# Gated linear attention: next pair's projections issued among this pair's heads, q, f and v in two buffers, merge gates kept in DRAM

## The chip, the cores and the metric

One Trainium2 chip, one core used. The metric is the device time of one execution in microseconds (us); the kernel before was run three times: median 4328.0 us, 4326.5 to 4329.1 us.

## The reference, cut to what matters

The program is two transformer blocks on 512 tokens of width 1024. The change lies in the second block's token mixer, which runs a delta-rule branch (finished before the changed code) and then the gated linear attention below, and merges the two:

```python
h = _modulate(_rmsnorm(x, norm1_w), sh1, sc1)          # 512 x 1024; hc: the same for 256 context tokens
qkv, ga, ab, qb, fb2, ib, gb, mg = split(h @ w_in)      # qb, ib, gb 1024 wide, fb2 and mg 2048
# _hgrn2_branch: 8 heads of 128, chunks of 64, forwards and backwards, context first
q = silu(qb); v = ib
f = lb + (1 - lb) * sigmoid(fb2);  logf = log(f);  k = 1 - f
bc = cumsum(logf, within a chunk)
scores = (q * exp(bc - ref)) @ (k * exp(ref - bc)).T, lower triangle
o = scores @ v + (q * exp(bc)) @ S;  S = exp(bc_last) * S + (k * exp(bc_last - bc)).T @ v
o = rmsnorm(o_forward + o_backward) * silu(gb)
# merge
g_a, g_b = split(sigmoid(mg));  mix = (g_a * (oa @ w_pa) + g_b * (ob @ w_pb)) @ w_o
```

## The kernel before, in words

All products of this stage are float32 split in a high and a low part, three matmuls for one (mm3, L308). `proj2` (L1208) projects the 512 tokens (and the 256 of the context where they are asked for) to up to 256 columns of w_in: it loads the weights through SP in pieces of 128x512 into three buffers w_raw (L1221), casts a piece to w_hi on ACT (L1224), subtracts on DVE, or on the engine given as `lo_eng`, to w_lo (L1225), both in two buffers, and accumulates in banks of a pool of four (`psa`): one bank for each 128 columns and one for the context. Then it evicts through a function that is handed in. `proj` (L313) is the same for 512 columns at once, in all four banks; of its w_lo pieces (L293) every fourth is done by POOL, the others by DVE.

`gla` (L1668) works on four pairs of heads (hg). For a pair it projects q (evicted with a tanh), the two directions' f (evicted by ACT as a sigmoid out of PSUM, L1711 and L1712, then scaled by DVE, L1713), takes the logarithms (L1732, four of 128x768, kept in the order of the code on ACT) and 1 - f (POOL, L1733), and projects v, which is transposed to token order. q, f and v have one buffer each. Then come the pair's two heads, and in each two directions d, four turns (j, d) in all. A turn scans the logarithms on DVE (L1755), makes the scaled copies of q and k (ACT's exponentials, POOL's L1764 and L1783, DVE's L1765), the scores, the transposed k, and runs a chain of 11 products and updates of the state S (PE L1811, DVE L1817). After two turns the head's output is summed (L1824, L1828), normalised on DVE (L1833 to L1839: gl_y), transposed (L1844), and multiplied by the gate, whose projection g is called once in a pair, after gl_y of head j = 0. At the end `split` makes obh and obl (ACT L274, DVE L275). After both heads `between(hg)` projects a quarter of the merge's gates, four tiles of 128x512 evicted with a tanh (L1906) which stay in SBUF, 16 tiles in all.

`block2_merge` (L1912) loads the delta-rule branch's output (oar, SP L1921), splits it (oah, oal), projects it with w_pa and ob with w_pb, and multiplies each result in PSUM by its gate (L1936, L1940).

The order of the code is not the order of issue: the framework (below: the planner) hands each engine its instructions beforehand in a fixed order, taking what it reckons ready, the code's order deciding between ready ones. `keep_in_program_order` pins an instruction behind the one that stands before it in the code on the same engine. Pools opened with `side="right"` share their memory with the right-hand pools opened after them, a tile of the new pool waiting for the last use of the old tiles that lie there.

Of the kernel before, what the change touches and what calls it, by code (L numbers as in the profile page):

```python
# [9 lines left out]
F32 = mybir.dt.float32  # L10
# [4 lines left out]
AF = mybir.ActivationFunctionType  # L15
ALU = mybir.AluOpType
# [4 lines left out]
P = 128  # L21
D = 1024
S = 512
# [155 lines left out]
class Net:  # L179
# [725 lines left out]
    def between(self):  # L905
        self.n_between += 1
        if self.n_between % 3 == 0:
            self.load_expert()
# [759 lines left out]
    def gla(self, acts, keep, between):  # L1668


        nc, a = self.nc, self.a
# [3 lines left out]
        main, ctx = acts  # L1675
        nw, ol, lb = self.gla_nw, self.gla_ol, self.gla_lb
        with ExitStack() as st:
# [19 lines left out]
            for hg in range(4):  # L1697
                q, f, gate = [], [[], []], []

                def q_ev(j, ps, pc):  # L1700
                    t = pool.tile([P, S], F32, tag=f"q{j}", name=f"glq{j}")
                    tc = self.to_cols(t)
                    nc.scalar.activation(out=tc, in_=self.by_rows(ps), func=AF.Tanh, scale=0.5)
                    stt(tc, tc, 1.0, self.by_rows(ps), op0=ALU.add, op1=ALU.mult)
                    q.append(t)

                def f_ev(d):
                    def g(j, ps, pc):
                        h = hg * 2 + j
                        t = pool.tile([P, 768], F32, tag=f"f{d}{j}", name=f"glf{d}{j}")  # L1710
                        nc.scalar.activation(out=self.to_cols(t[:, 0:512]), in_=self.by_rows(ps), func=AF.Sigmoid)  # L1711
                        nc.scalar.activation(out=t[:, 512:768], in_=pc, func=AF.Sigmoid)  # L1712
                        ts(t, t, ol[:, h:h + 1], lb[:, h:h + 1], op0=ALU.mult, op1=ALU.add)  # L1713
                        f[d].append(t)
                    return g

# [6 lines left out]
                self.proj2(4128 + hg * 256, 256, (main, None), q_ev)  # L1723
                self.proj2(5152 + hg * 256, 256, (main, ctx), f_ev(0))
                self.proj2(6176 + hg * 256, 256, (main, ctx), f_ev(1))

                lf = [[], []]
                for j in range(2):
                    for d in range(2):
                        t = tp.tile([P, 12, 64], F32, tag=f"lf{d}{j}", name="gl_lf", bufs=1)  # L1730
                        self.tc.keep_in_program_order(
                            nc.scalar.activation(out=t.rearrange("p c i -> p (c i)"), in_=f[d][j], func=AF.Ln))  # L1732
                        pts(f[d][j], f[d][j], -1.0, 1.0, op0=ALU.mult, op1=ALU.add)  # L1733
                        lf[d].append(t)

                v = pool.tile([P, 6, 256], F32, tag="v", name="glv")

                def v_ev(j, ps, pc):
                    t = tp.tile([P, 768], F32, tag="vT", name="gl_vT", bufs=1)
                    nc.scalar.copy(self.to_cols(t[:, 0:512]), self.by_rows(ps))  # L1740
                    nc.vector.tensor_copy(t[:, 512:768], pc)
                    for b0, nb in ((0, 4), (4, 2)):
                        pt = self.pt("pt_v")
                        for b in range(nb):
                            nc.tensor.transpose(pt[:, b * P:(b + 1) * P], t[:, (b0 + b) * P:(b0 + b + 1) * P], self.ident)
                        nc.vector.tensor_copy(v[:, b0:b0 + nb, j * P:(j + 1) * P], pt[:, :nb * P].rearrange("p (b c) -> p b c", c=P))
                self.proj2(7200 + hg * 256, 256, (main, ctx), v_ev)
                for j in range(2):
                    h = hg * 2 + j
                    Sst, qd = [], []  # L1750
                    for d in range(2):
# [66 lines left out]
                        Sst.append(S8)  # L1818
                    ss = tp.tile([P, 768], F32, tag="vT", name="gl_scs", bufs=1)[:, :512].rearrange("p (b i) -> p b i", b=NB)
# [30 lines left out]
                between(hg)  # L1850
# [39 lines left out]
    def block2_mix(self):  # L1890

        a, st, hT, hcT = self.a, self.st2, self.hT2, self.hcT
        oa_d = self.dram.tile([8, P, S], F32, name="oa_d")
        self.stx.close()
        self.banks(4, 0, 4)
        with self.pool("gdp") as gp:
            self.gdn((hT, hcT), gp, oa_d)

        self.banks(4, 2, 2)
        mgates = [[], [], [], []]  # L1900
        mp = st.enter_context(self.pool("mgp"))

        def merge_gates(n):
            def ev(j, ps):
                t = mp.tile([P, S], F32, name=f"mgate{n}{j}")
                self.nc.scalar.activation(out=self.to_cols(t), in_=self.by_rows(ps), func=AF.Tanh, scale=0.5)  # L1906
                mgates[n].append(t)
            self.proj(a["w_in_2"][0], 9248 + (n % 2) * 1024 + (n // 2) * 512, hT, True, ev)
        ob = self.gla((hT, hcT), mp, merge_gates)
        return st, mgates, oa_d, ob, self.xres  # L1910

    def block2_merge(self, st, mgates, oa_d, ob, xres):  # L1912
# [6 lines left out]
        for n in range(8):  # L1919
            raws.append(mr.tile([P, S], F32, tag=f"m2h{n}", name=f"oar{n}"))  # L1920
            nc.sync.dma_start(out=raws[n], in_=oa_d[n])  # L1921

# [500 lines left out]
```

## Time and profile before

| | |
|---|---|
| three runs | 4326.5, 4328.0, 4329.1 us |
| the profiled execution, its own time | 4329.5 us |
| its span, first to last instruction of the program | 4327.5 us |
| PE busy | 4021.8 us (93%) |
| DVE busy | 2740.9 us (63%) |
| ACT busy | 1682.5 us (39%) |
| POOL busy | 1156.9 us (27%) |

The span is what the trace covers; 2.0 us of the execution lie around it. Times in rows are counted from the span's start. A busy time counts when an engine works on an instruction; matmuls overlap, so a busy PE still has a clock that may be full (1.00) or half (0.50). Gated linear attention takes the stretch from about 2267 to 2793 us; the merge follows.

### The profile page before, as it was taken

Reading aid. Unit: us, or ns where it says so; the run is one execution under the profiler, and the core shown is the slowest. Engines: PE = TensorE matmul, PEld = TensorE weight load, DVE = VectorE, ACT = ScalarE, POOL = GpSimd, SP = SyncE. Lnnn points to the kernel's source line nnn. Section 1 sums busy time; section 2 is a strip of 40 time slices with the busy share of each in tenths; the row PEclk is TensorE's granted clock in tenths of the full one; section 3 lists DMA queues with packets and bytes.
Section 4 is the critical chain, followed back from the end, with each engine's and each line's share of the span. In section 5 each row is a group of like instructions: output and inputs, shape, how many; then the busy total and the mean of one; then the engine's idle time right before and its main releaser. Section 6 shows DMA issues by size and latency. Waiting matters only on the chain. (4 is left out here: it accounts for less than half of the span.)

```text
span 4327.5 us, 59112 instructions
## 1 busy us (share of the span) xinstructions
PE 4021.8 (93%) x21308; PEld 3134.1 (72%) x21309; DVE 2740.9 (63%) x6166; ACT 1682.5 (39%) x3200; POOL 1156.9 (27%) x1094
## 2 busy tenths in 40 slices
PE   8999899999998998899889899898789899999998
PEld 6677644767774456678777777676689799899886
DVE  5455455553644565777765655536989777777776
ACT  4544211544441144445543444323256333333333
POOL 2001100100021014222111211125779244444443
PEclk9999999999999998999989999999999999999999
DMA  4144698222458961212212111243145988888875
GB/s 137 30 121 141 248 419 357 91 79 81 112 190 329 420 245 49 65 49 57 57 46 57 47 52 52 66 127 117 59 161 198 331 310 293 302 295 301 289 267 195
DMA packets 342588, 739.72 MB, mean 171 GB/s; under 512 B 72513, under 2 KB 175025, under 8 KB 314641
## 3 DMA queue, kind: packets, MB, share of 16 engines
q1 hardware_dynamic: 277536, 540.54, 37.4%
q0 software_dynamic: 45376, 167.76, 10.4%
q10 hardware_dynamic: 19376, 27.57, 1.8%
q8 instruction: 171, 2.80, 0.3%
q14 instruction: 129, 1.05, 0.1%
HBM read 694.07 MB, written 41.70 MB: 170 GB/s over the span
## 5 line engine op out<-in xcount | busy, mean ns | idle before, releaser
L308 PE MATMUL acc<-rn_hi,w_lo 128*128 128x512 f32 x1224 | 506.7, 415 | 41.5 <-DVE w_lo L1225 15.2
L308 PE MATMUL acc<-rn_hi,w_hi 128*128 128x512 f32 x1224 | 507.7, 415 | 23.0 <-ACT w_hi L1224 13.2
L308 PE MATMUL acc<-rn_lo,w_hi 128*128 128x512 f32 x1224 | 500.9, 409 | 2.0 <-POOL rn_lo L275 2.0
L293 POOL TENSOR_TENSOR w_lo<-w_raw,w_hi 128x512 fp32r<-128x512 f32 x103 | 135.8, 1319 | 1041.4 <-ACT w_hi L291 828.4
L2246 ACT CAST p_hi<-p_raw 128x1024 fp32r<-128x1024 f32 x256 | 268.3, 1049 | 329.7 <-PE pu L308 236.3
L308 PE MATMUL pu<-rn_hi,p_lo 128*128 128x384 f32 x1024 | 349.7, 342 | 20.3 <-POOL p_lo L2247 16.0
L291 ACT CAST w_hi<-w_raw 128x512 fp32r<-128x512 f32 x316 | 196.0, 622 | 440.9 <-PE acc L308 339.9
L308 PE MATMUL pu<-rn_hi,p_hi 128*128 128x384 f32 x1024 | 347.5, 339 | 4.4 <-ACT p_hi L2246 3.2
L308 PE MATMUL pu<-rn_lo,p_hi 128*128 128x384 f32 x1024 | 347.1, 339 | 0.0
L2247 DVE TENSOR_TENSOR p_lo<-p_raw,p_hi 128x1024 fp32r<-128x1024 f32 x243 | 296.9, 1222 | 72.8 <-ACT p_hi L2246 72.8
L293 DVE TENSOR_TENSOR w_lo<-w_raw,w_hi 128x512 fp32r<-128x512 f32 x213 | 149.6, 703 | 264.6 <-ACT w_hi L291 253.6
L308 PEld LDWEIGHTS acc<-rn_hi,w_lo 128*128 128x128 f32 x1224 | 238.4, 195 | 105.0 <-POOL w_lo L293 18.9
L308 PE MATMUL py<-p_hi,ahi 128*128 128x512 f32 x768 | 304.4, 397 | 4.9 <-ACT ahi L274 3.1
L308 PE MATMUL py<-p_lo,ahi 128*128 128x512 f32 x768 | 304.5, 396 | 2.3 <-DVE p_lo L2247 2.3
L308 PE MATMUL py<-p_hi,alo 128*128 128x512 f32 x768 | 304.8, 397 | 0.1
L308 PEld LDWEIGHTS acc<-rn_hi,w_hi 128*128 128x128 f32 x1224 | 237.5, 194 | 68.1 <-ACT w_hi L1224 15.4
L308 PEld LDWEIGHTS acc<-rn_lo,w_hi 128*128 128x128 f32 x1224 | 237.7, 194 | 35.7 <-POOL rn_lo L275 3.2
L2236 POOL DMA_INDIRECT eu<-in_expert_v_dram,idx x128 | 190.1, 1485 | 266.0 <-DVE py L2140 249.6
L2236 POOL DMA_INDIRECT eu<-in_expert_u_dram,idx x128 | 178.5, 1395 | 278.2 <-DVE dots L2126 265.8
L963 PE MATMUL gu<-wgu,xe 128*64 128x512 f32 x1024 | 227.8, 597 | 0.0
L308 PEld LDWEIGHTS pu<-rn_hi,p_lo 128*128 128x128 f32 x1024 | 193.2, 189 | 27.2 <-POOL p_lo L2247 19.5
L308 PEld LDWEIGHTS pu<-rn_hi,p_hi 128*128 128x128 f32 x1024 | 193.4, 189 | 10.5 <-ACT p_hi L2246 4.9
(744 smaller groups left out, 9483.1 us busy)
## 6 DMA issues: line engine op xcount, KB each, us to landing
w_raw<-in_w_in_dram SPq DMA_DIRECT2D x336, 256.0 KB, 2.7
p_raw<-in_expert_u_T_dram SPq DMA_DIRECT2D x128, 512.0 KB, 3.7
p_raw<-in_expert_v_dram SPq DMA_DIRECT2D x128, 512.0 KB, 4.9
wgu<-in_w_exp_gate_dram SPq DMA_DIRECT2D x62, 1024.0 KB, 14.6
wgu<-in_w_exp_up_dram SPq DMA_DIRECT2D x62, 1024.0 KB, 17.6
wdn<-in_w_exp_down_dram SPq DMA_DIRECT2D x60, 1024.0 KB, 15.1
ada_w<-in_w_ada_dram SPq DMA_DIRECT2D x96, 256.0 KB, 3.2
gates_d<-gst ACTq DMA_DIRECT2D x24, 1024.0 KB, 4.6
```

The source lines that it names most:

```text
L291: self.nc.scalar.copy(hi, raw)
L293: eng.tensor_tensor(lo, raw, hi.bitcast(F32), op=ALU.subtract)
L308: self.nc.tensor.matmul(ps, l, r, start=st, stop=sp or shared, skip_group_check=shared)
L963: nc.tensor.matmul(gu[64 * e:64 * e + 64, :], xe[:, c, 64 * e:64 * e + 64], wgu[e][:, :, c, :], start=c == 0, stop=c == KC - 1)
L2236: self.nc.gpsimd.indirect_dma_start(out=t, out_offset=None, in_=rows, in_offset=bass.IndirectOffsetOnAxis(ap=idx, axis=0))
L2246: self.nc.scalar.copy(hi, raw)
L2247: (eng or self.nc.vector).tensor_tensor(lo, raw, hi.bitcast(F32), op=ALU.subtract)
```

## The change

The projections of q, f and v become a generator, `project`, with one projection for each step. Pair 0's four are done ahead of the loop. In pair hg, after each of the four turns, `next(nxt, None)` does one projection of pair hg + 1, and `between(hg)` does merge-gate tiles: one after each of the first three turns of a pair (none after the fourth), two after each turn of the last pair, until 16 are done. q, f and v get two buffers each. f is now evicted raw (ACT copies the 512 tokens, DVE the context), and at the head of its pair ACT does four sigmoids of 128x768 from SBUF, pinned one behind the other and behind what stands before them, ahead of the four logarithms. A merge-gate tile is a `proj2` of 128 columns (one bank, two weight pieces, each four row blocks of 128 columns wide, w_lo on POOL) instead of a quarter of a `proj`; its tile, one of two buffers, is written to DRAM through SP. The merge loads the 16 tiles back, through POOL's queue, at its beginning.

```diff
@@ -1668,6 +1668,7 @@
     def gla(self, acts, keep, between):
 
 
         nc, a = self.nc, self.a
         tt, ts, stt = nc.vector.tensor_tensor, nc.vector.tensor_scalar, nc.vector.scalar_tensor_tensor
         ptt, pts = nc.gpsimd.tensor_tensor, nc.gpsimd.tensor_scalar
@@ -1694,11 +1695,10 @@
             for t in (sc, kn, xh):
                 nc.gpsimd.memset(t, 0.0)
             res = []
-            for hg in range(4):
-                q, f, gate = [], [[], []], []
+            def project(hg, q, f, vs):
 
                 def q_ev(j, ps, pc):
-                    t = pool.tile([P, S], F32, tag=f"q{j}", name=f"glq{j}")
+                    t = pool.tile([P, S], F32, tag=f"q{j}", name=f"glq{j}", bufs=2)
                     tc = self.to_cols(t)
                     nc.scalar.activation(out=tc, in_=self.by_rows(ps), func=AF.Tanh, scale=0.5)
                     stt(tc, tc, 1.0, self.by_rows(ps), op0=ALU.add, op1=ALU.mult)
@@ -1706,36 +1706,16 @@
 
                 def f_ev(d):
                     def g(j, ps, pc):
-                        h = hg * 2 + j
-                        t = pool.tile([P, 768], F32, tag=f"f{d}{j}", name=f"glf{d}{j}")
-                        nc.scalar.activation(out=self.to_cols(t[:, 0:512]), in_=self.by_rows(ps), func=AF.Sigmoid)
-                        nc.scalar.activation(out=t[:, 512:768], in_=pc, func=AF.Sigmoid)
-                        ts(t, t, ol[:, h:h + 1], lb[:, h:h + 1], op0=ALU.mult, op1=ALU.add)
+                        t = pool.tile([P, 768], F32, tag=f"f{d}{j}", name=f"glf{d}{j}", bufs=2)
+                        nc.scalar.copy(self.to_cols(t[:, 0:512]), self.by_rows(ps))
+                        nc.vector.tensor_copy(t[:, 512:768], pc)
                         f[d].append(t)
                     return g
 
-                def g_ev(j, ps, pc):
-                    t = tp.tile([P, S], F32, tag=f"gb{j}", name="gl_gate", bufs=1)
-                    tc = self.to_cols(t)
-                    nc.scalar.activation(out=tc, in_=self.by_rows(ps), func=AF.Tanh, scale=0.5)
-                    stt(tc, tc, 1.0, self.by_rows(ps), op0=ALU.add, op1=ALU.mult)
-                    gate.append(t)
-                self.proj2(4128 + hg * 256, 256, (main, None), q_ev)
-                self.proj2(5152 + hg * 256, 256, (main, ctx), f_ev(0))
-                self.proj2(6176 + hg * 256, 256, (main, ctx), f_ev(1))
-
-                lf = [[], []]
-                for j in range(2):
-                    for d in range(2):
-                        t = tp.tile([P, 12, 64], F32, tag=f"lf{d}{j}", name="gl_lf", bufs=1)
-                        self.tc.keep_in_program_order(
-                            nc.scalar.activation(out=t.rearrange("p c i -> p (c i)"), in_=f[d][j], func=AF.Ln))
-                        pts(f[d][j], f[d][j], -1.0, 1.0, op0=ALU.mult, op1=ALU.add)
-                        lf[d].append(t)
-
-                v = pool.tile([P, 6, 256], F32, tag="v", name="glv")
-
                 def v_ev(j, ps, pc):
+                    if j == 0:
+                        vs.append(pool.tile([P, 6, 256], F32, tag="v", name="glv", bufs=2))
                     t = tp.tile([P, 768], F32, tag="vT", name="gl_vT", bufs=1)
                     nc.scalar.copy(self.to_cols(t[:, 0:512]), self.by_rows(ps))
                     nc.vector.tensor_copy(t[:, 512:768], pc)
@@ -1743,8 +1723,39 @@
                         pt = self.pt("pt_v")
                         for b in range(nb):
                             nc.tensor.transpose(pt[:, b * P:(b + 1) * P], t[:, (b0 + b) * P:(b0 + b + 1) * P], self.ident)
-                        nc.vector.tensor_copy(v[:, b0:b0 + nb, j * P:(j + 1) * P], pt[:, :nb * P].rearrange("p (b c) -> p b c", c=P))
-                self.proj2(7200 + hg * 256, 256, (main, ctx), v_ev)
+                        nc.vector.tensor_copy(vs[0][:, b0:b0 + nb, j * P:(j + 1) * P], pt[:, :nb * P].rearrange("p (b c) -> p b c", c=P))
+                yield self.proj2(4128 + hg * 256, 256, (main, None), q_ev)
+                yield self.proj2(5152 + hg * 256, 256, (main, ctx), f_ev(0))
+                yield self.proj2(6176 + hg * 256, 256, (main, ctx), f_ev(1))
+                yield self.proj2(7200 + hg * 256, 256, (main, ctx), v_ev)
+            made = [], [[], []], []
+            for _ in project(0, *made):
+                pass
+            for hg in range(4):
+                (q, f, vs), made = made, ([], [[], []], [])
+                v, gate, nxt = vs[0], [], project(hg + 1, *made) if hg < 3 else iter(())
+                def g_ev(j, ps, pc):
+                    t = tp.tile([P, S], F32, tag=f"gb{j}", name="gl_gate", bufs=1)
+                    tc = self.to_cols(t)
+                    nc.scalar.activation(out=tc, in_=self.by_rows(ps), func=AF.Tanh, scale=0.5)
+                    stt(tc, tc, 1.0, self.by_rows(ps), op0=ALU.add, op1=ALU.mult)
+                    gate.append(t)
+                jd = [(j, d) for j in range(2) for d in range(2)]
+                for j, d in jd:
+                    h = hg * 2 + j
+                    t = f[d][j]
+                    self.tc.keep_in_program_order(nc.scalar.activation(out=t, in_=t, func=AF.Sigmoid))
+                    ts(t, t, ol[:, h:h + 1], lb[:, h:h + 1], op0=ALU.mult, op1=ALU.add)
+                lf = [[], []]
+                for j, d in jd:
+                    t = tp.tile([P, 12, 64], F32, tag=f"lf{d}{j}", name="gl_lf", bufs=1)
+                    self.tc.keep_in_program_order(
+                        nc.scalar.activation(out=t.rearrange("p c i -> p (c i)"), in_=f[d][j], func=AF.Ln))
+                    pts(f[d][j], f[d][j], -1.0, 1.0, op0=ALU.mult, op1=ALU.add)
+                    lf[d].append(t)
                 for j in range(2):
                     h = hg * 2 + j
                     Sst, qd = [], []
@@ -1816,6 +1827,8 @@
                                 else:
                                     stt(dst, src, tot[:, c:c + 1], kv, op0=ALU.mult, op1=ALU.add)
                         Sst.append(S8)
+                        next(nxt, None)
+                        between(hg)
                     ss = tp.tile([P, 768], F32, tag="vT", name="gl_scs", bufs=1)[:, :512].rearrange("p (b i) -> p b i", b=NB)
                     ptt(ss, sc[:, 0], sc[:, 1], op=ALU.add)
                     o = self.tr("gl_o").rearrange("p (b d) -> p b d", b=NB)
@@ -1847,7 +1860,6 @@
                     lo = keep.tile([P, S], F32R, name=f"obl{h}")
                     self.split(hi, lo, gate[j])
                     res.append((hi, lo))
-                between(hg)
         return res
 
     def block2_open(self):
@@ -1897,19 +1909,30 @@
             self.gdn((hT, hcT), gp, oa_d)
 
         self.banks(4, 2, 2)
-        mgates = [[], [], [], []]
         mp = st.enter_context(self.pool("mgp"))
 
-        def merge_gates(n):
-            def ev(j, ps):
-                t = mp.tile([P, S], F32, name=f"mgate{n}{j}")
+        mg_d = self.dram.tile([4, 4, P, S], F32, name="mg_d")
+        def merge_gate(n, j):
+            def ev(_, ps, pc):
+                t = mp.tile([P, S], F32, tag="mgate", name="mgate_t", bufs=2)
                 self.nc.scalar.activation(out=self.to_cols(t), in_=self.by_rows(ps), func=AF.Tanh, scale=0.5)
-                mgates[n].append(t)
-            self.proj(a["w_in_2"][0], 9248 + (n % 2) * 1024 + (n // 2) * 512, hT, True, ev)
-        ob = self.gla((hT, hcT), mp, merge_gates)
-        return st, mgates, oa_d, ob, self.xres
-
-    def block2_merge(self, st, mgates, oa_d, ob, xres):
+                self.nc.sync.dma_start(out=mg_d[n, j], in_=t)
+            self.proj2(9248 + (n % 2) * 1024 + (n // 2) * 512 + j * P, P, (hT, None), ev, self.nc.gpsimd)
+        todo = [(n, j) for n in range(4) for j in range(4)]
+        turns = [0]
+        def between(hg):
+            turns[0] += 1
+            for _ in range((turns[0] % 4 != 0) if hg < 3 else 2):
+                if todo:
+                    merge_gate(*todo.pop(0))
+        ob = self.gla((hT, hcT), mp, between)
+        assert not todo
+        return st, mg_d, oa_d, ob, self.xres
+    def block2_merge(self, st, mg_d, oa_d, ob, xres):
         nc, a = self.nc, self.a
         tt, stt = nc.vector.tensor_tensor, nc.vector.scalar_tensor_tensor
         mst, ost = ExitStack(), ExitStack()
@@ -1919,6 +1942,10 @@
         for n in range(8):
             raws.append(mr.tile([P, S], F32, tag=f"m2h{n}", name=f"oar{n}"))
             nc.sync.dma_start(out=raws[n], in_=oa_d[n])
+        mgates = [[op.tile([P, S], F32, name=f"mgate{n}{j}") for j in range(4)] for n in range(4)]
+        for n in range(4):
+            for j in range(4):
+                nc.gpsimd.dma_start(out=mgates[n][j], in_=mg_d[n, j])
 
         def next_oa():
             n = len(oa)
```

## Rows read from the trace of the kernel before

**Rows 1.** The page's head: span, and each engine's busy time, share and instructions.
```profile
span 4327.5 us, 59112 instructions
PE 4021.8 (93%) x21308; PEld 3134.1 (72%) x21309; DVE 2740.9 (63%) x6166; ACT 1682.5 (39%) x3200; POOL 1156.9 (27%) x1094
```

**Rows 2.** Windows, PE alone: stretch, length, PE busy (instructions), granted clock, DMA share, GB/s.
```profile
2267.00:2793.00 526.00, 471.87 (x2676) 0.95 0.19 54
2356.00:2414.00 58.00, 51.20 (x274) 0.94 0.17 46
2500.00:2560.00 60.00, 53.27 (x283) 0.94 0.18 49
2646.00:2706.00 60.00, 54.13 (x286) 0.91 0.18 49
2706.00:2793.00 87.00, 70.85 (x421) 0.93 0.22 67
```

**Rows 3.** Waits of PE, 2267 to 2793: waiter, releaser: us, times, longest.
```profile
PE acc L308 <- DVE w_lo L1225: 12.8, 6, 3.6
PE pt_o L1844 <- DVE gl_y L1839: 11.9, 5, 4.6
PE acc L308 <- ACT w_hi L1224: 5.8, 3, 1.9
PE acc L308 <- DVE w_lo L293: 2.2, 4, 0.9
```

**Rows 4.** Timeline of PE between pairs 0 and 1: start, us, instruction, [idle before].
```profile
2393.59 0.50 PE L308 MATMUL acc<-rn_hi,w_hi 128*128 128x512 f32 x1 [1.94 <-ACT w_hi L1224]
...
2398.60 0.79 PE L308 MATMUL acc<-rn_hi,w_lo 128*128 128x512 f32 x1 [3.59 <-DVE w_lo L1225]
```

**Rows 5.** Timeline of ACT in the same place.
```profile
2388.69 1.28 ACT L1732 ACT_TABLE_LOAD   x1
2389.98 3.05 ACT L1732 ACTIVATE gl_lf<-glf 128x768 f32<-128x768 f32 x4
2392.93 1.12 ACT L1224 CAST w_hi<-w_raw 128x512 fp32r<-128x512 f32 x2
```

**Rows 6.** Timeline of DVE in the same place.
```profile
2390.86 3.99 DVE L1755 TENSOR_TENSOR_SCAN gl_lf<-reset,gl_lf 128x768 f32<-128x768 f32 x2 [1.15 <-ACT gl_lf L1732]
...
2397.24 2.99 DVE L1225 TENSOR_TENSOR w_lo<-w_raw,w_hi 128x512 fp32r<-128x512 f32 x2
```

**Rows 7.** Timeline of PE at the end of head j = 0 of pair 1.
```profile
2457.73 0.39 PE L308 MATMUL acc<-rn_hi,w_lo 128*128 128x512 f32 x1
2457.96 0.39 PE L308 MATMUL acc<-rn_hi,w_hi 128*128 128x512 f32 x1
2460.69 0.85 PE L1844 MATMUL pt_o<-ident,gl_y 128*128 128x128 f32 x3 [2.34 <-DVE gl_y L1839]
```

**Rows 8.** Timeline of PE at the end of the last pair, rows with idle time.
```profile
2775.39 0.87 PE L1811 MATMUL pt_kv<-glv,gl_kn 128*128 128x128 f32 x4 [1.16 <-DVE gl_S L1817]
...
2789.26 1.11 PE L1844 MATMUL pt_o<-ident,gl_y 128*128 128x128 f32 x4 [4.59 <-DVE gl_y L1839]
2792.39 2.07 PE L308 MATMUL acc<-oah,w_hi 128*128 128x512 f32 x4 [2.01 <-ACT oah L274]
```

**Rows 9.** The delta-rule branch, 1750 to 2140: w_lo on POOL (lines), PE's wait.
```profile
L1225 POOL TENSOR_TENSOR w_lo<-w_raw,w_hi 128x512 fp32r<-128x512 f32 x36 | 52.1, 1450 | 82.4 <-ACT w_hi L1224 82.4
...
PE acc L308 <- POOL w_lo L1225: 6.2, 4, 1.9
```

**Rows 10.** Timeline of POOL between pairs 0 and 1.
```profile
2390.92 7.09 POOL L1733 TENSOR_SCALAR glf<-glf 128x768 f32<-128x768 f32 x4 [63.55 <-ACT gl_lf L1732]
2397.98 1.70 POOL L1764 TENSOR_TENSOR gl_e<-glq,gl_e 128x512 f32<-128x512 f32 x1
```

**Rows 11.** Timeline of POOL in the merge: a weight piece, and an issue of a load.
```profile
2797.26 1.29 POOL L293 TENSOR_TENSOR w_lo<-w_raw,w_hi 128x512 fp32r<-128x512 f32 x1 [24.30 <-ACT w_hi L291]
...
2924.08 0.56 POOL L257 DMA_DIRECT2D arow<-mod_d  x1
```

## The prediction

> **What bounds the kernel now.** I read the page's head first: PE is busy 93% of the span, every other engine 63% or less [rows 1], so a gain has to come from PE's idle time or from its clock, since the change takes no matmul away. Next the windows, to see what is there to gain in the stage that changes [rows 2]. Of its 526.0 us PE works 471.9, so it idles 54.1; its mean clock is 0.95, so 526 x 0.05 = 26.3 us go to stretches at half clock. 80 us, 1.9% of the kernel, are the most that any reordering of this stage can give. Of these the three stretches in which pair 1's, 2's and 3's projections run alone have 6.8 + 6.7 + 5.9 = 19.4 us of idle time and 58 x 0.06 + 60 x 0.06 + 60 x 0.09 = 12.5 us of lost clock; the last pair's 87 us have 16.2 us idle and 6.1 of clock. Then PE's waits, which name the causes [rows 3]: weight pieces not cast in time (12.8 for w_lo, 5.8 for w_hi, and 2.2 in the merge-gate projections), and 11.9 us for gl_y, the normalised head output.
>
> The timelines say why. Between pairs, ACT loads a table (1.28) and does four logarithms in one go (3.05), and only then the casts that the v projection waits for [rows 5]; DVE does two scans (3.99) and more before it subtracts the pieces [rows 6]. PE stands 1.94 and 3.59 us [rows 4]. At the end of head j = 0 the g projection has run out before gl_y is there: 2.34 us [rows 7], and much the same in pairs 2 and 3. At the very end the state's chain has nothing beside it (1.16 us is its longest wait; the seven waits of the chain make 3.8), then come 4.59 and 2.01 us [rows 8].
>
> Two matmul starts of 512 columns lie 0.23 us apart [rows 7]. A merge-gate tile is 8 x 3 = 24 of them, 5.6 us; one weight piece of it, or of the q or g projection, feeds 12, 2.8 us; a piece of f or v feeds 12 more of half the columns, 4.2 us.
>
> **The change, part by part.**
>
> *Projections among the heads.* PE's work stays. What is new is that PE always has a projection to do beside a head, since q, f and v of the next pair no longer wait for this pair's buffers. The seven of the last pair's merge tiles (3 x 3 = 9 are gone by then) are 39 us of such work where the old order had four, 22 us. So the 2.34 us at the ends of heads j = 0, 7.0 in three pairs, should go (bounds 0 and 7.0): I take 6. Of the last chain's 3.8 us I take 3 (0 to 3.8). The 4.59 and 2.01 stay: there the last head has only its own tail, and oah waits for memory.
>
> *The head of a pair.* The projections no longer stand alone, but a batch on ACT remains and doubles: a table, four sigmoids, a table, four logarithms. A sigmoid of 128x768 is not in the trace; by the logarithms of that shape four cost 3.05 [rows 5], which I take, and the end of the range is the doubled price. The batch is 2 x (1.28 + 3.05) = 8.7 us, in which no cast is done. Two pieces are cast ahead: 5.6 us of PE for q, g and merge tiles, 8.4 for f and v. A cast is half of 1.12 [rows 5], a subtraction about 0.7 on DVE, so the gap is 8.7 + 1.3 - 5.6 = 4.4 or 8.7 + 1.3 - 8.4 = 1.6; I take 3.0. Three times 3.0 instead of 19.4 gains 10.4, less 3.0 for pair 0, whose sigmoids and logarithms so far lie under the delta-rule branch's matmuls and are now pinned behind v's eviction: 7.4. Bounds: 19.4 if the planner slips casts between, 0 if scans and casts meet as in [rows 6].
>
> *Clock.* 26.3 us of clock go with 54.1 of idle time, 0.49 for each. Less idle time by 7.4 + 6 + 3 = 16.4 brings back 8.0 (0 to 15).
>
> *Evictions.* f's raw copy takes ACT as long as its sigmoid did; the context's half moves to DVE, 16 copies of half a tile. DVE and ACT are hidden under PE as long as PE is the bound; if that cover goes, a batch more on ACT is the 4.3 us of a pair, 17 in four, which the rival below contains.
>
> *Merge tiles.* 32 pieces instead of 32, but all w_lo on POOL. The same form stands in the delta-rule branch: 36 pieces at 1450 ns, for which PE waited 6.2 us [rows 9]. 32 / 36 of this is 5.5, in place of the 2.2 of [rows 3]: minus 3.3. Bounds: nothing, and 32 x 0.75 = 24, were each piece's extra time on the path. POOL has room, 27% in the span [rows 1]; behind a piece on its queue are gl_e and gl_qd, for which scores wait.
>
> *The 16 writes.* Each waits on SP for its tanh, with the next loads of w_raw queued behind it. A load has three buffers and two cast pieces before PE (5.6 us or more) to hide this; I take 0. If that cover is gone a write costs a tanh, about as long as w_lo's 1.45, 16 x 1.45 = 23 us. The merge's 16 loads back are issued by POOL at 0.56 us each [rows 11], 9.0 us, after the last tiles in that memory are done, near 2790. Behind them waits the weight piece that POOL subtracted at 2797.26 for 1.29 us [rows 11]. PE comes to it three pieces after 2792.4, at 2800.8; POOL is there at 2790 + 9.0 + 1.3 = 2800.3. I take 1 us (0 to 15). The gates themselves are wanted after 96 matmuls, 22 us on.
>
> *Sum.* 7.4 + 6 + 3 + 8.0 - 3.3 - 1 = 20 us. The profiled execution took 4329.5 us (span 4327.5 and 2.0 around it), so 4309.5 by it. The median of three runs is 1.5 below it: I predict 4308.
>
> *A rule against the loads.* Three loads that POOL issued in a row take 0.56 us each at most with DVE at work [rows 11]. The Trainium skill, "SBUF — State Buffer", section "SBUF: two separate sides", says that a DMA issued from POOL's queue has its descriptors written by the GpSimd cores, which a DVE instruction in a two-port mode locks out. Its next section has such a DMA at 3.1 us instead of 0.62; 16 would hold POOL 50 us by it.
>
> **The rivals.**
>
> (a) *The batch starves PE.* The sigmoids are pinned behind obh, the last thing of the pair before, and the next scores need the batch and POOL's 1 - f: 1.28 + 3.05 + 1.28 + 0.76, then 7.09 and 1.70 [rows 5, 10], 15.2 us without head work. If the four banks or the two cast buffers allow PE only 5.6 us of it, four heads of pairs idle 9.6 us and lose some 3.4 of clock, 52 us against 32 (19.4 + 12.5) now: 20 slower, 4.3 of costs, against 6 + 3 + 4.4 of the tails: 4329.5 + 11, some 4341. It decides from 10 us a pair's head, clock included. For it: today half this batch costs 6 us of idle time [rows 4, 5]. Against: today PE has one projection there and now merge tiles and the next q as well.
>
> (b) *Nothing changes.* The planner already fills heads with whatever is ready, as the g projection's matmuls right up to gl_y show [rows 7]; the casts wait as before, only the tails gain, 9 + 4.4 of clock, and 4.3 of costs and 3 for pair 0 come off: 4323. This is also the case that the change doesn't spread what it says: projections issued late, where buffers are let go.
>
> (c) *PE stays fed.* Of 19.4 + 7.0 + 3.8 us all goes, with 15 of clock, less 4: 4288, at most some 4280. For it: 60% busy DVE and ACT below that leave room. Against: chains that do not change, gl_S and the end.
>
> (d) *POOL held by its loads.* If each issue waits out a DVE subtraction of 0.7 as well, 16 x 1.26 = 20 us, PE stands some 11 at the merge's first projection: 4320. The skill's rule named above would make this 40 and the whole 4349.
>
> **How the numbers follow.** Two measurements of this kernel can be told apart from 0.2% on, 8.7 us: faster is below 4319, slower above 4337. The forecast's own range, 4297 to 4319, has 0.43; (c) 0.14; (b) 0.21; (a) 0.17; (d) 0.05, most of it within 0.2%. Faster: 0.43 + 0.14 = 0.57, and 0.01 of (d). Within: 0.21 + 0.03 = 0.24. Slower: 0.17 + 0.01 = 0.18. The range leaves out half of (c)'s far end and half of (a), 4278 to 4341.
>
> **What would show it.** The stretches in which L308 runs alone for 58 us are gone, pt_kv and acc alternating all through; PE's idle time in the stage falls from 54 to near 40 and its clock rises to 0.96 or 0.97. PE's waits for gl_y fall from 11.9 to about 6, those for w_lo and w_hi from 18.6 to about 12, with the rest sitting right at the sigmoids; a new wait for POOL's w_lo of about 5 appears. In the merge, a wait for POOL's w_lo at its fourth piece tells of (d). The prediction is wrong if PE idles over 6 us at a pair's head with two cast pieces used up (a), if the waits for w_lo and w_hi are as large as before (b), or if the time goes to a stage that the change does not touch.

## The result, and the profile after

The changed kernel took 4357.6 us (median of 4 runs, 4354.7 to 4365.4) against 4327.8 us before (4326.5 to 4329.1): ratio 1.0067, 95% interval 1.0055 to 1.0078. It is slower by 24 to 34 us; 4308 was forecast, and the range ended at 4341. The profiled execution took 4356.8 us, its span 4354.5.

The page's head, in answer to [rows 1]: PE's busy time fell by 7.5 us, while the span grew by 27.0. PE does not work longer, it stands longer.

```profile
span 4354.5 us, 59190 instructions
PE 4014.3 (92%) x21308; PEld 3136.8 (72%) x21309; DVE 2737.1 (63%) x6158; ACT 1692.1 (39%) x3200; POOL 1207.5 (28%) x1134
```

Windows of PE, in answer to [rows 2]: the whole stage, four stretches at the heads of the pairs, and the rest of the kernel.

```profile
2266.00:2815.00 549.00, 456.80 (x2652) 0.91 0.21 61
2273.00:2283.00 10.00, 4.12 (x12) 0.50 0.00 1
2414.00:2438.00 24.00, 4.71 (x21) 0.58 0.08 22
2561.00:2585.00 24.00, 4.71 (x21) 0.58 0.08 22
2709.00:2733.00 24.00, 5.19 (x23) 0.63 0.06 18
...
2815.00:4354.00 1539.00, 1445.78 (x7273) 0.98 0.67 231
```

The stage is 23.0 us longer (526.0 before). PE idles 92.2 us of it, 38.1 more than before, while its busy time is 15.1 less: 24 matmuls fewer fall into the window (5.6 us at 0.23), and the rest I could not separate. In three windows of 24 us, one at the head of each of pairs 1, 2 and 3, it works only 4.7 to 5.2 us. The rest of the kernel is 5 us longer (4354.5 - 2815 = 1539.5 against 4327.5 - 2793 = 1534.5); of the change only the loads back of the gates reach into it, and the cause is open.

The waits of PE in the stage, in answer to [rows 3], name the reason:

```profile
PE pt_s L1787 <- DVE gl_x L1776: 52.8, 7, 16.0
PE acc L308 <- ACT w_hi L1224: 11.0, 1, 11.0
PE pt_s L1789 <- DVE gl_xh L1781: 10.6, 4, 3.3
PE pt_o L1857 <- DVE gl_y L1852: 9.4, 3, 4.6
```

The old waits for the weight pieces of q, f and v are gone, and so is most of the wait for gl_y at heads j = 0. In their place the first scores of a pair (pt_s) wait 16 us for gl_x, the scaled keys, and then 3.3 us for gl_xh, a copy of half of them. Here is that place at the head of pair 1, as [rows 4] showed it before, in PE's timeline:

```profile
2413.98 0.39 PE L308 MATMUL acc<-rn_hi,w_lo 128*128 128x512 f32 x1
2430.38 0.66 PE L1787 MATMUL pt_s<-gl_e,gl_x 128*128 128x64 f32 x2 [16.01 <-DVE gl_x L1776]
2434.32 0.69 PE L1789 MATMUL pt_s<-gl_e,gl_xh 128*128 128x64 f32 x2 [3.28 <-DVE gl_xh L1781]
```

ACT at the same time, in answer to [rows 5]:

```profile
2410.77 0.62 ACT L274 CAST obh<-gl_gate 128x512 fp32r<-128x512 f32 x1 [2.31 <-DVE gl_gate L1858]
2411.40 1.28 ACT L1749 ACT_TABLE_LOAD   x1
2412.70 3.04 ACT L1749 ACTIVATE glf<-glf 128x768 f32<-128x768 f32 x4
2415.76 1.28 ACT L1756 ACT_TABLE_LOAD   x1
2417.05 3.04 ACT L1756 ACTIVATE gl_lf<-glf 128x768 f32<-128x768 f32 x4
2420.11 1.28 ACT L1793 ACT_TABLE_LOAD   x1
...
2424.47 1.08 ACT L1703 ACTIVATE glq<-acc 128x512 f32<-128x512 f32 x1
...
2427.53 1.16 ACT L1224 CAST w_hi<-w_raw 128x512 fp32r<-128x512 f32 x2
```

And what follows the logarithms on DVE and POOL (compare [rows 6, 10]):

```profile
2417.93 3.99 DVE L1766 TENSOR_TENSOR_SCAN gl_lf<-reset,gl_lf 128x768 f32<-128x768 f32 x2 [1.47 <-ACT gl_lf L1756]
...
2425.80 2.82 DVE L1766 TENSOR_TENSOR_SCAN gl_lf<-reset,gl_lf 128x768 f32<-128x768 f32 x1
2428.55 1.69 DVE L1776 TENSOR_TENSOR gl_x<-glf,gl_x 128x512 f32<-128x512 f32 x1
```

```profile
2417.98 7.09 POOL L1757 TENSOR_SCALAR glf<-glf 128x768 f32<-128x768 f32 x4 [16.98 <-ACT gl_lf L1756]
...
2426.97 2.72 POOL L1775 TENSOR_TENSOR gl_e<-glq,gl_e 128x512 f32<-128x512 f32 x1
```

Read from the top: the sigmoids stand right behind obh, the last output of pair 0. From there sigmoids, logarithms, scans and scaled copies run one behind the other for 19.0 us (2411.40 to 2430.38) before the first score of pair 1 can start. PE has work for only the first 3.0 of them: it finishes a projection at 2414.4, the next instruction in its fixed order is the score, and the next weight piece is cast by ACT at 2427.53, behind the batch and the exponentials, 16.1 us after the batch began.

### The profile page after: what moved, and what is told of

The parts are those of the page before. It is cut to its first block, busy times and chain, and to the rows that moved or that the text cites. A ratio compares the mean times of both kernels' runs of the same rounds, so it can differ in the third digit from the quotient of the medians.

```text
span 4354.5 us, 59190 instructions
## 1 busy us (share of the span) xinstructions
PE 4014.3 (92%) x21308; PEld 3136.8 (72%) x21309; DVE 2737.1 (63%) x6158; ACT 1692.1 (39%) x3200; POOL 1207.5 (28%) x1134
## 5 line engine op out<-in xcount | busy, mean ns | idle before, releaser
L293 POOL TENSOR_TENSOR w_lo<-w_raw,w_hi 128x512 fp32r<-128x512 f32 x95 | 125.6, 1323 | 933.7 <-ACT w_hi L291 792.5
L291 ACT CAST w_hi<-w_raw 128x512 fp32r<-128x512 f32 x284 | 175.9, 621 | 395.7 <-PE acc L308 297.1
L293 DVE TENSOR_TENSOR w_lo<-w_raw,w_hi 128x512 fp32r<-128x512 f32 x189 | 133.2, 705 | 256.3 <-ACT w_hi L291 240.3
L308 PEld LDWEIGHTS acc<-rn_lo,w_hi 128*128 128x128 f32 x1224 | 237.6, 194 | 38.4 <-POOL rn_lo L275 3.2
L1224 ACT CAST w_hi<-w_raw 128x512 fp32r<-128x512 f32 (+1 forms) x177 | 109.3, 621 | 296.2 <-PE acc_c L308 111.1
## 6 DMA issues: line engine op xcount, KB each, us to landing
wgu<-in_w_exp_gate_dram SPq DMA_DIRECT2D x62, 1024.0 KB, 15.1
```

The source lines that it names most:

```text
L291: self.nc.scalar.copy(hi, raw)
L293: eng.tensor_tensor(lo, raw, hi.bitcast(F32), op=ALU.subtract)
L308: self.nc.tensor.matmul(ps, l, r, start=st, stop=sp or shared, skip_group_check=shared)
L1224: nc.scalar.copy(hi, raw)
```

## The experiments

Ratios are to the kernel before, with 95% intervals. My theory after the two traces: the pinned batch behind obh, with PE's next instruction waiting for it, costs the time (theory T in the expectations, theory B in the later ones). The rivals: the merge gates' new path (M), and the second buffers (B in the first four). The kernel before was measured again beside these runs; its medians lie from 4329.2 to 4332.2 us.

**The pins taken off.** Sigmoids and logarithms stay where they are in the code; the planner places them freely.

```diff
-  self.tc.keep_in_program_order(nc.scalar.activation(out=t, in_=t, func=AF.Sigmoid))
+  nc.scalar.activation(out=t, in_=t, func=AF.Sigmoid)
   (the logarithms likewise)
```

> The changed kernel without the two pins on sigmoids and logarithms; all work the same. T, if the pin is what holds the batch behind the last head: the planner takes the sigmoids as f arrives, PE's wait at pt_s falls from 16 us to under 8, 4320 to 4345. T, if it is their place in the code alone: same batch, same place, 4352 to 4360. B and M: 4355 to 4360.

Measured: 4321.8 us, 0.9978 [0.9967, 0.9988]. Two pins removed make a faster kernel of a slower one, 36 us below the changed kernel. Waits of PE there:

```profile
PE pt_o L1856 <- DVE gl_y L1851: 21.4, 8, 5.3
PE pt_s L1786 <- DVE gl_x L1775: 5.6, 2, 2.9
```

The wait for gl_x falls from 52.8 to 5.6 us, while gl_y rises from 9.4 to 21.4.

**Only the sigmoids' pin taken off.**

```diff
-  self.tc.keep_in_program_order(nc.scalar.activation(out=t, in_=t, func=AF.Sigmoid))
+  nc.scalar.activation(out=t, in_=t, func=AF.Sigmoid)
   (the logarithms stay pinned)
```

> The changed kernel with the pin taken from the four sigmoids alone; the logarithms stay pinned. Theory B (length of the pinned batch behind the last output sets the wait): the sigmoids go into the pair before, the logarithms stay a batch of 4.3 us: pt_s waits some 11.7 us and the time is that of sigmoids at eviction, 4338 to 4346. Rival L (it is the sigmoids' pin alone that holds the start of the chain; once they are free the logarithms follow at once): near the kernel without any pin, 4320 to 4330.

Measured: 4311.0 us, 0.9954 [0.9939, 0.9969]: the mechanism of rival L, some 9 us below its range, and my form of the theory missed. A pin holds an instruction behind the one that stands before it in the code. For the first sigmoid that is obh of the pair before; for the logarithms it is a sigmoid, and once the sigmoids are free the logarithms go with them. ACT in pair 0, some 50 us ahead of pair 1's first score (2412.0):

```profile
2358.74 1.28 ACT L1749 ACT_TABLE_LOAD   x1
2360.04 0.85 ACT L1749 ACTIVATE glf<-glf 128x768 f32<-128x768 f32 x1
2360.79 0.60 ACT L1224 CAST w_hi<-w_raw 128x512 fp32r<-128x512 f32 x1
2361.30 0.84 ACT L1749 ACTIVATE glf<-glf 128x768 f32<-128x768 f32 x1
2362.16 1.28 ACT L1756 ACT_TABLE_LOAD   x1
2363.45 0.84 ACT L1756 ACTIVATE gl_lf<-glf 128x768 f32<-128x768 f32 x1
```

Both run in short pieces with casts between, soon after f is evicted. There are 21 table changes in the stage instead of 10, and the stage is faster. Why it came out below the kernel with no pins (the intervals overlap a little) I did not test.

**A shorter batch.** f is evicted as a sigmoid again; only the logarithms are left at the head, pinned.

```diff
-  nc.scalar.copy(self.to_cols(t[:, 0:512]), self.by_rows(ps))
-  nc.vector.tensor_copy(t[:, 512:768], pc)
+  nc.scalar.activation(out=self.to_cols(t[:, 0:512]), in_=self.by_rows(ps), func=AF.Sigmoid)
+  nc.scalar.activation(out=t[:, 512:768], in_=pc, func=AF.Sigmoid)
+  ts(t, t, ol[:, h:h + 1], lb[:, h:h + 1], op0=ALU.mult, op1=ALU.add)
```

> The changed kernel with the sigmoid and its scaling back at the eviction out of PSUM, so that the batch at the head of a pair is one table and four logarithms, 4.3 us instead of 8.7. T: PE's idle time there falls from 19 us by 4 to 5 in each of four pairs, 4335 to 4345, less what more table loads take back. B or M: unchanged, 4355 to 4360.

Measured: 4343.4 us, 1.0022 [1.0009, 1.0035], with PE's longest wait as foretold (first row). Then with a tanh for the sigmoid, which needs no table change at the evictions (func=AF.Tanh, scale=0.5, ol halved and lb + ol/2 in its place):

> The changed kernel with f evicted as tanh(x/2), which is in the set of the exponentials, and the constants made for it: the pinned batch is only a table and four logarithms (4.3 us instead of 8.7), and no eviction changes the table. Theory B: pt_s waits about 11.7 us at each head of a pair as in the kernel that evicts f as a sigmoid, and ACT's table changes at the evictions lie under PE's work anyway, so the time is the same as there: 4338 to 4346. Rival T, the table changes: if the sigmoids at the evictions held casts back, their removal gives 5 to 15 us more: 4328 to 4338.

Measured: 4337.1 us, 1.0008 [0.9993, 1.0023]; its row of the same wait is the second below. A batch of 8.7 us: wait 16.0; one of 4.3 us: wait 11.7. The 4.4 us taken out of the batch come off the wait almost whole (4.3), so nothing covers that part of it. The wait is as theory B has it in both; the tanh's median lies just below B's range and inside that of rival T, but its interval overlaps the sigmoid's, so what the table changes at evictions cost is not settled; by the medians it is 6 us.

```profile
PE pt_s L1783 <- DVE gl_x L1772: 34.7, 6, 11.7
```

```profile
PE pt_s L1785 <- DVE gl_x L1774: 35.7, 6, 11.7
```

**The pinned batch in another place.** Pins kept, the batch cut in two by head: the next pair's head j = 0 behind turn (1, 0), head j = 1 behind turn (0, 0) of its own pair.

```diff
   next(nxt, None)
   between(hg)
+  if (j, d) == (0, 0): prepare(hg, 1, f, lf)
+  if (j, d) == (1, 0) and hg < 3: prepare(hg + 1, 0, made[1], lf_next)
```

> The changed kernel with the pinned batch cut in two by head and issued a turn earlier: the two sigmoids and logarithms of the next pair's head j = 0 behind turn (1, 0), those of head j = 1 behind turn (0, 0); pins kept, lf of j = 0 in two buffers. Theory B, the place of the pinned batch (behind the last output of a pair, with PE's next instruction in order waiting for what it makes): the waits of pt_s for gl_x of 16 us go, since a whole turn of PE's work lies behind each half batch; of the 36 us that taking the pins off gave, 25 or more come back: 4320 to 4332. Rival P, the pins themselves (any pinned group on ACT holds the casts of the weight pieces behind it, wherever it stands): eight table changes more, the same lost time in smaller pieces: 4345 to 4360.

Measured: 4315.0 us, 0.9962 [0.9948, 0.9977], faster than theory B asked for, and rival P is out: the same instructions, pinned, with more table changes. The wait for gl_x:

```profile
PE pt_s L1787 <- DVE gl_x L1776: 1.5, 4, 0.5
```

**The merge gates through memory, alone.** The kernel before, with only the merge gates changed: four tiles of 128 columns between each two pairs, w_lo on POOL, written out and loaded back.

```diff
-  ob = self.gla((hT, hcT), mp, merge_gates)
+  def between(hg):
+      for _ in range(4):
+          merge_gate(*todo.pop(0))
+  ob = self.gla((hT, hcT), mp, between)
```

> The kernel before with only the merge gates' part of the change (16 tiles projected singly, w_lo on POOL, written to DRAM, read back in the merge), four tiles at the end of each pair. Theory T (the batch of sigmoids and logarithms at the head of a pair, pinned behind the pair before, starves PE): this part is nearly free, 4326 to 4334 us against 4328. Rival M (the merge gates' new path costs the time: POOL's subtractions, SP's writes, POOL's 16 loads): 4343 to 4358.

Measured: 4343.7 us, 1.0023 [1.0012, 1.0034]: some 10 us slower, where the prediction had 4.3 for these edits. My theory, by which this part is nearly free, missed, and the time is at the lower end of rival M's range. The kernel before has 8 of its 32 subtractions on POOL (L293), so this run has 24 more there. The same with w_lo on DVE:

```diff
-  self.proj2(9248 + ..., P, (hT, None), ev, self.nc.gpsimd)
+  self.proj2(9248 + ..., P, (hT, None), ev)
```

> The kernel before with the merge's gates through memory, four tiles between each two pairs, as the run that did this alone, but with their w_lo subtracted on DVE instead of POOL. Theory G (POOL's subtraction, 1.37 us instead of 0.75 on DVE, and what queues behind it on POOL cost that run's 10 us): 4328 to 4334. Rival D (the path through memory costs them: the tanh's own write in SP's queue ahead of the loads of weights, and the single tile between writes): 4338 to 4346, with the waits for gl_y still near 19 us.

Measured: 4324.5 us, 0.9986 [0.9972, 1.0000], below the range of either theory. The intervals are apart: 0.37%, 16 us, for 32 subtractions on POOL. The path through memory itself costs nothing that shows. The stage in windows of PE, first of the kernel with POOL, then of that with DVE:

```profile
2244.00:2801.00 557.00, 491.93 (x2757) 0.94 0.22 62
```

```profile
2245.00:2787.00 542.00, 482.00 (x2756) 0.95 0.24 68
```

And PE's waits in the same order:

```profile
PE pt_o L1844 <- DVE gl_y L1839: 19.3, 5, 4.6
PE acc L308 <- DVE w_lo L1225: 11.5, 6, 3.6
...
PE acc L308 <- POOL w_lo L1225: 4.2, 7, 1.0
```

```profile
PE acc L308 <- DVE w_lo L1225: 15.1, 9, 3.6
PE pt_o L1844 <- DVE gl_y L1839: 11.2, 6, 4.6
```

Of the 15 us, PE's idle time makes 65.1 - 60.0 = 5, and its busy time 10; it works 53.2 us of the stage at a granted clock of 0.50, against 32.5, and half the difference is those 10. The waits for w_lo, on POOL and DVE together, are alike, 15.7 and 15.1 us; the difference is in the waits for gl_y, 19.3 and 11.2. Here is why, in DVE's timeline ahead of one gl_y in the run with POOL, and POOL's beside it:

```profile
2609.74 1.21 DVE L268 TENSOR_TENSOR rq_t<-gl_rs 128x4 f32<-128x4 f32 x1
2610.99 1.18 DVE L269 SCALAR_TENSOR_TENSOR rq_t<-rq_t,gl_ms 128x4 f32<-128x4 f32 x1
2612.21 0.16 DVE L270 SCALAR_TENSOR_TENSOR gl_rs<-rq_t,gl_rs 128x4 f32<-128x4 f32 x1
```

```profile
2608.08 2.85 POOL L1225 TENSOR_TENSOR w_lo<-w_raw,w_hi 128x512 fp32r<-128x512 f32 x2 [2.63 <-ACT w_hi L1224]
2610.89 1.27 POOL L1764 TENSOR_TENSOR gl_e<-glq,gl_e 128x512 f32<-128x512 f32 x1
```

The normalisation that leads to gl_y is a chain of DVE instructions of 128x4 (L265 to L270). They take 0.16 us each where POOL is idle and about 1.2 beside its work; over the stage they sum to 31.2 us with w_lo on POOL and to 18.1 with it on DVE, 13 less, while PE's waits for gl_y fall by 8.

**The second buffers, alone**, added to the kernel with the merge gates through memory (bufs=2 for q, f and v; code order as before).

> e1 and two buffers for q, f and v, the code's order as in the kernel before (sigmoid at the eviction, logarithms before v). T: no batch is pinned behind a pair's last head, so nothing is lost: 4308 to 4332. Rival B (buffers and early projections themselves cost it, by banks and casts that the heads have to share): 4343 or more. If the planner does not use the buffers by itself it is e1 again within 3 us.

Measured: 4344.9 us, 1.0029 [1.0019, 1.0039], the same as without them. Buffers cost nothing and bring nothing while the code calls the projections between the pairs.

**DVE for POOL in the changed kernel**, the pins as they are; the edit is the one-word one above.

> The changed kernel with one word changed: the merge tiles' w_lo subtracted on DVE instead of POOL; pins as they are. Theory of two costs that add: the 16 us of POOL's subtractions go, the four waits at the heads of pairs stay 16 us: 4338 to 4346. Rival F (cover among the heads; the waits at the heads end with DVE's gl_x, which now has 32 subtractions more ahead of it): 4352 to 4362.

Measured: 4354.2 us, 1.0057 [1.0040, 1.0074]: rival F's range, and not apart from the changed kernel (1.0055 to 1.0078). PE's waits for gl_x are as long as there, 53.3 us. That what is off the path can't be won where PE stands at the heads anyway is my reading; no run isolates it.

**Versions that draw on both.** The sigmoids unpinned, w_lo on DVE:

> The changed kernel with the pins taken from the sigmoids and the merge tiles' w_lo subtracted on DVE instead of POOL. Theory: two costs that add, the pinned sigmoids (46 us of the profiled execution when freed) and POOL's subtractions (16 us in the old order of the code). With both gone: 4293 to 4303. Rival F (where the projections lie among the heads, POOL's longer subtraction has cover and DVE is the busier one): the same as with the sigmoids' pins off alone, 4306 to 4316.

Measured: 4303.6 us, 0.9937 [0.9921, 0.9954], just above the range for two costs that add and below that for cover (the 46 us in the expectation are a difference of medians; the profiled executions differ by 50); its interval overlaps that of the same kernel with POOL (0.9939 to 0.9969), so this pair does not decide. The early batch, w_lo on DVE:

> The kernel with the pinned batch cut in two and issued a turn earlier, with the merge tiles' w_lo on DVE instead of POOL. Theory of two costs that add: 4297 to 4308. Rival F (POOL's subtraction has cover among the heads): 4310 to 4320, as with the early batch alone.

Measured: 4295.7 us, **0.9919 [0.9903, 0.9935]**, the fastest of all, 28 to 42 us below the kernel before. The two costs add here, the time even a little below that range: against the early batch with POOL the intervals are apart. The early batch with f as a tanh (w_lo on POOL):

> Early batch in two halves, and f evicted as tanh, so that a half batch is a table and two logarithms (2.9 us) instead of 5.7. If the length of a pinned group still costs something where a turn of PE's work lies behind it, this is 5 to 10 us faster than the early batch with sigmoids: 4303 to 4311; if only its place counts, the same: 4311 to 4319.

Measured: 4301.7 us, 0.9936 [0.9921, 0.9952], on the side of a length that costs; but its interval touches that of the early batch with sigmoids, so this stays open. The fastest kernel's stage, in windows of PE and in PE's waits:

```profile
2260.00:2765.00 505.00, 463.40 (x2682) 0.97 0.24 67
```

```profile
PE pt_o L1861 <- DVE gl_y L1856: 8.3, 5, 4.6
```

PE idles 41.6 us against 54.1 [rows 2], and its clock is 0.97 against 0.95; the longest single wait left is that of the last output, 4.6 us as before [rows 8].

## Why the prediction was wrong

*The head of a pair: the step that failed.* "I take 3.0" a pair stood against 16.0 + 3.3 measured, and pair 0, for which I took 3.0, has 11.0 for a cast behind the batch and 4.0 for gl_x. The first three rows of PE's waits, nearly all of them at these four heads, sum to 74.4 us where the old boundaries had 19.4 of idle time. The parts of the step were right: four sigmoids take 3.04 (3.05 taken), the batch 8.7. Three readings were not. First, I ended PE's wait with a cast right after the batch; ACT casts 7.4 us later (2420.09 to 2427.53), behind exponentials and the next q's tanh. Second, I counted projections as cover from which PE could choose. Its order is fixed beforehand: the next q's matmuls were spent on the tail of the head before, up to 2414.4, and then pt_s stands next. That matmuls run in the order of the program is also what the Trainium skill, "TensorE: Matmul & The Clock Gate", section "Step-by-step: what each phase is for", says; the trace agrees, with 16.01 us of idle time ahead of pt_s and a merge tile behind it. But that tile's first piece is cast only at 2427.53, some 2 us before the score is ready, so in any order of PE's it could have filled no more than these 2 of the 16 us: the cast stands behind the batch as well. At pair 0 a projection does stand ahead of pt_s, and it starves for its cast. Third, I did work out the chain from obh to the next scores, 15.2 us, but as a rival's; it is 19.0, and 3.0 of it were covered.

Of the miss of 47 us (4309.5 forecast for the profiled execution, 4356.8 measured) this step alone makes 62: 7.4 gained against 74.4 - 19.4 = 55 lost. The other terms together came out some 15 better than forecast. Outside the heads PE's idle time fell from 54.1 - 19.4 = 34.7 to 92.2 - 74.4 = 17.8, by 17, where my terms gave 6 + 3 - 3.3 - 1 = 4.7; its busy time fell by 15.1, where I had 8.0 of clock; and the rest of the kernel took 5 back. No step of mine gave these.

*Rival (a)* is what happened, and its mechanism is shown: a shorter batch shortens the wait by as much, and another place or no pin takes it away. My price of it, 4341, was 16 us too low: it gave each head 9.6 us of idle time, 38.4 in four. What I held against it, merge tiles and the next q beside the batch, was what the code calls there, not what PE's queue holds there.

*Projections among the heads.* At heads j = 0, 7.0 us of gl_y waits were to shrink by 6: in the pairs 1 and 2 they are gone, in the last pair 2.85 is left, and a new one of 1.99 stands at the end of pair 2's second head. The last chain's seven waits make 4.2 us before, not the 3.8 of the prediction, and 1.3 after: 2.9 less (3 taken). The second held, the first by a third to two thirds.

*Clock.* 8.0 us were to come back; 1.5 did. The stretches of the stage with a granted clock of 0.50 sum to 51.5 us before and 98.4 after, but PE works only 39.1 and 36.3 us in them and loses half of that, 19.6 and 18.1. A lower clock costs only where PE works: my 26.3 us, length times missing clock, counted idle time a second time. The four windows at the heads show it best: by length they would have lost 5 + 10 + 10 + 9 = 34 us, but PE worked only 18.7 us there and can have lost 9.4 at most.

*Merge tiles.* I took 3.3 and bounded it by 24. In the changed kernel the cost can't be told from nothing (1.0057 against 1.0067), in the old order it is 16 us, and in the early-batch version 0.43%, 19 us. I took it from PE's waits for POOL by name [rows 9]; in the old order these are 4.2 us, about what the waits for DVE's w_lo grow by when POOL has none, and the cost that can be named sits in the waits for gl_y. That view was too narrow.

*The 16 writes and the loads back.* POOL issues the loads where the merge begins, and the piece behind them waits for ACT, not for them:

```profile
2812.70 4.22 POOL L1948 DMA_DIRECT2D mgate<-mg_d  x8 [3.29 <-PE pt_o L1857]
2821.13 1.29 POOL L293 TENSOR_TENSOR w_lo<-w_raw,w_hi 128x512 fp32r<-128x512 f32 x1 [4.20 <-ACT w_hi L291]
```

The 16 loads take 0.54 us each, one 0.61, and 1 us was allowed for them; rival (d) is out. The rule of the Trainium skill, "SBUF — State Buffer", section "SBUF: two separate sides", that a DVE instruction in a two-port mode locks out the descriptors of such a load, does not show in these issues. It is not tested by them either: beside them DVE did updates of S and subtractions (oal), and the trace does not say whether any of it ran in such a mode. The 3.1 us that the section behind it gives are for the whole transfer, whose landing the trace does not give here, and not for the time that POOL is held, as the 50 us of the prediction took them. The writes, 16 in the stage, are not apart from noise: with DVE for POOL the path through memory alone is at 0.9986.

*The rivals (b) and (c).* The order did change, so (b) is out. (c)'s 4288 is approached only when batch and POOL are both moved: 4295.7.

## What to carry to other kernels

Where instructions are pinned, ask behind what: the instruction that precedes the first of them in the code sets the start of all that follows it, and here it was the very last output of the pair before. When a step is cut loose from its loop so that its work can be done ahead, the steps that consume it have to be moved too; the projections went a pair ahead, while their sigmoids stayed at the head. And cover is what stands ahead of the waiting instruction in the engine's own queue, with its inputs already made, not what the code issues nearby.

## What the runs showed of the hardware that was not expected

Table changes on ACT, 1.28 us each, cost little where they are spread: 10 in the changed kernel's stage, 30 in that of the kernel without pins, which is 36 us faster. A weight piece's subtraction takes POOL 1.37 us on average in the run with the merge gates alone, DVE 0.74 in the one with DVE; moving 32 of them takes 44 us off POOL and puts 24 on DVE, the busier of the two, and is faster by 16. DVE is not busier for it, 322.9 us of the stage with w_lo on POOL and 322.4 with it on DVE: its other work gets shorter by as much.

POOL's subtraction does not have one duration. In the timeline of POOL in the changed kernel, at the head of pair 1 and late in the last pair:

```profile
2429.65 4.46 POOL L1225 TENSOR_TENSOR w_lo<-w_raw,w_hi 128x512 fp32r<-128x512 f32 x2
...
2784.46 1.29 POOL L1225 TENSOR_TENSOR w_lo<-w_raw,w_hi 128x512 fp32r<-128x512 f32 x1 [2.42 <-ACT w_hi L1224]
```

It takes 1.29 where DVE only updates S, and 2.23 a piece where DVE has scans and scaled copies to do; DVE's scan in its turn took 2.82 beside POOL's scaled copies (2425.80), and its 128x4 instructions 1.2 instead of 0.16 (above). The Trainium skill, "SBUF — State Buffer", section "Who interferes with whom", says that a DVE instruction with two inputs in SBUF and a GpSimd instruction that reads SBUF keep each other out. These rows agree with it. The chain to gl_y accounts for 8 us of PE's waits by name; that the whole 16 us come from this was not isolated by a run.
